# The down product of a bidirectional encoder layer: the first pair's weight parts at two places modulo 256 bytes, and its first matmul whole

## The chip, the cores and the metric

The kernel runs on one core of a Trainium2 chip. The metric is the device time of one execution in microseconds (us). It is measured several times; the median of three runs of the kernel before is 824.79 us. One more execution was taken with the profiler, and all views of the profile and the trace below come from it.

TensorE multiplies a stationary operand of 128x128, which a weight load puts into the array, with a moving operand of up to 512 columns. The profile shows the two as separate instructions: PE is the matmul, PEld the weight load. DVE is VectorE, ACT is ScalarE, POOL is GpSimd, and SP is SyncE, which starts the loads of weights.

## The reference

The kernel computes one layer of an encoder for 512 rows (tokens) of 1024 values. A mixing part (retention and a gated spatial unit) comes first; the change concerns the feed-forward part at the end:

```python
def _conv_gated_mlp(h, w_up, conv_w, conv_b, w_down):
    hid = h @ w_up
    c = hid.shape[-1]
    hid = lax.conv_general_dilated(
        hid, conv_w.reshape(CONV_W, 1, c), window_strides=(1,),
        padding=((CONV_W // 2, CONV_W // 2),),
        dimension_numbers=('NWC', 'WIO', 'NWC'), feature_group_count=c) + conv_b
    a, b = jnp.split(hid, 2, axis=-1)
    return (jax.nn.gelu(a) * b) @ w_down
...
        h2 = _rmsnorm(x, g_pre_ffn)
        x = x + _rmsnorm(_conv_gated_mlp(h2, w_up, conv_w, conv_b, w_down), g_post_ffn)
```

Here h is 512 x 1024, w_up is 1024 x 5632, w_down is 2816 x 1024, and all is float32. The last matrix product, with w_down, is called the down product.

## The kernel before

**Two parts for each number.** Every float32 operand is split into a high part, rounded to the matmul's format, and a low part, the rest (`split`, lines 89 to 91: ScalarE writes the high part in line 84, VectorE subtracts in line 91). A product a x w is then three matmuls: high x high, high x low, low x high. So matmuls come in threes throughout.

**Weights.** All weights lie in DRAM as 146 blocks of 128 x 1024 values. `w_get` hands them out in order and keeps some blocks ahead of the use; SyncE loads a block into one of four raw buffers, ScalarE and VectorE write the parts into slots. There are nine slots of 128 x 1088 values (`slot`, lines 128 and 129), used in turn. A slot is a little larger than a block needs, so that its content can begin at an offset, `at`, given in values of 4 bytes. A row of a slot is 4352 bytes, 17 times 256, so the slots all begin at the same place modulo 256 bytes; the blocks that hold activations are 2048 bytes, 8 times 256. In the program as built, slots and activation blocks alike begin at 64 modulo 256. The place of an operand modulo 256 bytes is therefore 64 plus four times its offset:

- the first up products, called early (`w_block`, line 144; L949 calls the three matmuls of L229 to L231): offset 16, both parts at 128;
- the products of `Pair` (`w_form`, lines 174 to 177; `product`, L688), which the gates, u and the up product use: the low part has offset 16, place 128, and the high part has offset 528 or 560, place 128 or 0. u's first four forms have 560; u's later forms and the first four of the first gate have 528, all later ones 560;
- the down product (`w_down`, L197, and `w_block`, L144): offset 48, both parts at 0;
- activations and what is derived from them: 64.

**The order of the matmuls.** In `Pair.product` and in the early products the weights are stationary and the activations move. In the down product it is the other way: activations are stationary and the weight parts move. A `Pair` runs two 128 x 512 output blocks with seven products of quarter size each in place of eight; its products are 256 columns wide. Between them stand whole up blocks with 512 columns (L957).

**The down product.** The output is made in two halves of 512 columns. Of the 22 row blocks of w_down, 18 are taken in nine pairs (`DP`); the other four are `whole` blocks, two for each half. For a pair, `w_down` writes a slot pair for the unit "q" (three quarters of the weight block pair, as they are) and one for the unit "t" (four sums and differences of quarters, which VectorE makes in L190 to L195). The tile of the high part is named dh, that of the low part dl. `products` (L1077) then runs seven units, each for two halves of 128 rows and three matmuls, 42 matmuls of 256 columns a pair, into seven sums in PSUM. `add_whole` (L1098) adds the whole blocks, L1109: in the first half they follow pairs 4 and 6, in the second they come at the end. After each half VectorE combines the seven sums (`steps`, L1122 to L1129 and L1171 to L1179). At the very end, rows are scaled and written out, four row blocks in the order 0, 2, 1, 3 (L1207 to L1238).

**What the change touches.** `w_down`'s offset, L197, and the split of the first matmul in `products`, L1089 to L1095: where `lead` is set (the first half), the first matmul of all is issued as two, one of 16 columns and one of 240, with the same stationary operand. `lead` also caps how far `w_get` looks ahead in the last pair (L1080).

Of the kernel before, what the change touches and what calls it, by code (L numbers as in the profile page):

```python
# [32 lines left out]
DOWN0 = NW - NF  # L33
DP = 9
# [15 lines left out]
def tile_block(ctx: ExitStack, tc, xT, x, wall, par, cs, wsp, bsp, gpost, gpre, gffn, out):  # L50
    nc = tc.nc
# [6 lines left out]
    def nm(s):  # L58
        uid[0] += 1
        return f"{s}_{uid[0]}"  # L60

    def blk(dt=F32, n="blk", shape=(P, S)):
        return sb.tile(list(shape), dt, tag="blk", bufs=NBLK, name=nm(n))
# [4 lines left out]
    def tmp(n="tmp", shape=(P, S)):  # L68
        return sb.tile(list(shape), F32, tag="tmp", bufs=6, name=nm(n))
# [7 lines left out]
    def ps(shape=(P, S)):  # L77
        return pp.tile(list(shape), F32, tag="ps", name=nm("ps"))
# [4 lines left out]
    def copy(o, i):  # L83
        nc.scalar.activation(out=o, in_=i, func=AF.Copy)  # L84

    def as32(t):
        return t.bitcast(F32)

    def split(hi, lo, src):
        copy(hi, src)  # L90
        return nc.vector.tensor_sub(lo, src, as32(hi))  # L91
# [7 lines left out]
    i = 0  # L99
    while i < NW:  # L100
# [7 lines left out]
        elif i == UP0 + 2 * COUPLES[0][0]:  # L108
# [3 lines left out]
            i = UP0 + 2 * COUPLES[-1][1] + 2  # L112
# [12 lines left out]
    def raw_tile():  # L125
        return sb.tile([P, 1024], F32, tag="raw", bufs=4, name=nm("raw"))

    def slot(n, at=0, w=1024):
        return sb.tile([P, 1088], F32R, tag="w4", bufs=9, name=nm(n))[:, at : at + w]
# [51 lines left out]
    def w_down(form, i):  # L181

        if form == "q":
            raw = w_raw["q"] = raw_tile()
            nc.sync.dma_start(raw, wall[i])
            raw = raw[:, : 3 * 256]
        else:
            b, raw = w_raw["q"], raw_tile()
            two = "p (n c) -> p n c"
            nc.vector.tensor_tensor(  # L190
                out=raw[:, :512].rearrange(two, n=2), in0=b[:, :512].rearrange(two, n=2),
                in1=b[:, None, 768:].to_broadcast([P, 2, 256]), op=ALU.add,
            )
            nc.vector.tensor_add(raw[:, 512:768], raw[:, :256], b[:, 256:512])
            nc.vector.tensor_add(raw[:, 768:], raw[:, 512:768], b[:, 512:768])  # L195
        w = 768 if form == "q" else 1024
        hi, lo = slot("dh", 48, w), slot("dl", 48, w)  # L197
        if w_behind:
            copy(hi, raw)
            with tc.issue_after(w_behind[0]):  # L200
                nc.vector.tensor_sub(lo, raw, as32(hi))
        else:
            w_low[form, i] = split(hi, lo, raw).ins
        return hi, lo
# [4 lines left out]
    def w_size(u):  # L209
        return 2 if u[0] in ("blk", "q", "t") else 1  # L210

    def w_next():
        u = units[w_pos[1]]
        w_ready[w_pos[1]] = w_unit(u)
        w_pos[1] += 1
        return w_size(u)

    def w_get(look=LOOK, most=99):

        i = w_pos[0]  # L220
        w_pos[0] += 1
        room = 2 * look + (2 if w_size(units[i]) == 2 else 0)
        n = sum(w_size(u) for u in units[i : w_pos[1]])
        while w_pos[1] < len(units) and (w_pos[1] <= i or n + w_size(units[w_pos[1]]) <= min(most, max(room, 9 if look == LOOK else 0))):
            n += w_next()
        return w_ready.pop(i)
# [53 lines left out]
    for k in range(KD):  # L280
# [6 lines left out]
        wh, wl = w_get(1 if k < 4 else LOOK)  # L287
# [11 lines left out]
        for m in range(8):  # L299
            c = slice(m * P, (m + 1) * P)  # L300
# [78 lines left out]
    for m in range(8):  # L379
        t = blk(n="qkraw")  # L380
# [8 lines left out]
    for t in range(NT):  # L389
# [4 lines left out]
            start=True,  # L394
            stop=True,
# [252 lines left out]
    for n, acc in enumerate(t_group()):  # L648
        if n < 2:
            for k in (n + 2, n + 6):  # L650
                t = tmp("xT")
# [93 lines left out]
    for j in range(KD // 2):  # L745
        p = Pair(AF.Gelu_apprx_tanh, lambda: blk(n="u"), scale=rbc)
# [204 lines left out]
    def up_block(between=None):  # L951
        (wh, wl), o = w_get(), ps()
        for k in range(KD):
            if between and k == KD // 2:
                between()
            c = slice(k * P, (k + 1) * P)
            mm3(o, wh[:, c], wl[:, c], *h2(k, slice(0, S)), k == 0, k == KD - 1)  # L957
        return o
# [90 lines left out]
    i = 0  # L1049
    while i < NF:  # L1050
        if i in couples:
            p = Pair(None, lambda: tmp("c"), h2, h2forms)
            p.part1()
            o = [up_block()]
# [5 lines left out]
        else:  # L1060
            o = []
# [12 lines left out]
    M1, M2, M3, M5, M6, M7, M4, M8 = range(8)  # L1074
    whole = []

    def products(m, j, steps={}, lead=False):  # L1077
        for n, (unit, at, act) in enumerate(UNITS):
            if n in (0, 3):
                wh, wl = w_get(most=9 if lead and j == DP - 1 else 99)  # L1080
            if j == 0 and n not in m:
                m[n] = ps()
            f = slice(at * 256, (at + 1) * 256)
            ah, al = dforms[j][act]
            for t in range(2):
                c = slice(t * P, (t + 1) * P)
                o = m[n][:, t * 256 : (t + 1) * 256]
                for i, (a_, w_) in enumerate(((ah, wh), (ah, wl), (al, wh))):
                    first = j == t == i == 0  # L1089
                    cuts = (0, 16, 256) if lead and first and n == 0 else (0, 256)  # L1090
                    for p, q in zip(cuts, cuts[1:]):
                        nc.tensor.matmul(  # L1092
                            o[:, p:q], a_[:, c], w_[:, f][:, p:q], start=first and p == 0,
                            stop=j == DP - 1 and i == 2 and n not in (M2, M3, M4), skip_group_check=True,
                        )  # L1095
            steps.get(n, lambda: None)()

    def add_whole(m, t, g, w, last=False, banks=(0, 1)):  # L1098
# [16 lines left out]
    m = {}  # L1115
# [10 lines left out]
    def after4(yy=yy):  # L1126
# [4 lines left out]
    steps = {  # L1131
        M1: lambda: copy(e1, m[M1]),
        M2: lambda: v.tensor_add(c11, m[M2], e1),
        M3: lambda: copy(e3, m[M3]),
        M6: lambda: v.tensor_add(uu, m[M6], e1), M7: after7,
    }
    for j in range(DP):
        products(m, j, steps if j == DP - 1 else {}, True)
        if j + 1 < DP:
            with tc.issue_after(w_low["t", DOWN0 + j + 1]):  # L1140
                for kind, i in {0: later[:1], 1: later[1:3], 2: later[3:4], 3: later[4:6], 4: later[6:7], 5: later[7:]}.get(j, ()):
                    if kind == "w":
                        whole.append(two_parts(gp[2 * DP + i], i > 1))
                    else:
                        down_forms(i)
        if j in (3, 5):
            w = w_get()
            for t in range(NT):
                add_whole(m, t, j // 2 - 1, w, j == 5)
            if j == 5:  # L1150
                copy(c22, m[M8])
# [16 lines left out]
    m = {n: m[o] for n, o in ((M1, M8), (M2, M1), (M3, M2), (M5, M3), (M6, M6), (M7, M5), (M4, M7), (M8, M4))}  # L1168
# [10 lines left out]
    steps = {M1: lambda: copy(e1, m[M1]), M6: after6, M7: after7}  # L1179
    for j in range(DP):  # L1180
        products(m, j, steps if j == DP - 1 else {})
        if j == 0:
            w_behind.clear()
            after4()
        if 1 < j < 2 + NT:
            first_share(j - 2)
# [20 lines left out]
    for t in (0, 2, 1, 3):  # L1207
# [12 lines left out]
        for i, (b, e) in enumerate((((M2, e1), (M3, xx)), ((M4, uu), (M8, yy)))[t // 2]):  # L1220
            f, h = slice((t % 2) * 256, (t % 2 + 1) * 256), slice(i * 256, (i + 1) * 256)
# [139 lines left out]
```

## Time and profile before

| | |
|---|---|
| median of three runs | 824.79 us (823.5 to 825.1) |
| the profiled execution's own time | 824.38 us |
| its span, first to last instruction | 822.6 us |
| mean granted clock of TensorE | 0.998 |
| down product, start of the first matmul to start of the last | 702.49 to 814.13 us |
| from there to the end of the span | 8.5 us |

How to read it: the span is what the trace covers, and 1.8 us of the profiled execution lie around it. The granted clock is the share of TensorE's clock that the chip let through; 1.00 is full. A step is the time from the start of one matmul to the start of the next. The chain of work that ended last follows the last instruction back to what released it, step by step; where it names TensorE, the time between two entries is made of such steps. In the table by window, a matmul that only reaches into the window is counted too.

### The profile page before, as it was taken

The page shows a single profiled execution, that of the slowest core. Times are in us where ns is not written, and L with a number is a line of the kernel's source. Part 1 is how long each engine was busy: PE and PEld are TensorE (multiplying, and loading weights), DVE is VectorE, ACT ScalarE, POOL GpSimd, SP SyncE. Part 2 cuts the span into 40 slices and gives each one's busy share as a digit, 9 for nine tenths or more (in the row PEclk, how much of TensorE's full clock was granted, in tenths as well). Part 3 has the DMA queues.
Part 4 walks back from the last instruction along what each step waited for, and adds up shares of the span by engine and source line. Part 5 has one row for each costly group of instructions (what it writes and reads, how often), then busy time and mean ns, then how long its engine had stood idle before and what let it go on. Part 6 is the DMA issues. An engine that isn't in the chain of part 4 may idle for free.

```text
span 822.6 us, 13205 instructions
## 1 busy us (share of the span) xinstructions
PE 812.9 (99%) x5153; PEld 733.7 (89%) x5153; DVE 658.5 (80%) x1076; ACT 431.2 (52%) x733; POOL 103.9 (13%) x108
## 2 busy tenths in 40 slices
PE   9999999999999999999999999999999999999996
PEld 7888888888999999999988898999999998999995
DVE  7579897878898787767765589679899899898956
ACT  6636445536665444444444566456566566555532
POOL 0100000103221111132221211111111100000002
PEclk9999999999999999999999999999999999999999
DMA  8733222213233333223359111233333341334334
GB/s 287 255 116 103 77 78 77 77 52 93 75 105 127 103 103 102 80 101 103 125 165 364 64 58 50 100 103 103 103 103 103 103 154 53 102 103 128 105 129 129
DMA packets 29247, 93.76 MB, mean 114 GB/s; under 512 B 3392, under 2 KB 4032, under 8 KB 29184
## 3 DMA queue, kind: packets, MB, share of 16 engines
q1 hardware_dynamic: 26784, 86.58, 31.9%
q0 software_dynamic: 1968, 6.03, 2.5%
q8 instruction: 40, 0.66, 0.3%
q10 hardware_dynamic: 432, 0.30, 0.1%
q14 instruction: 23, 0.19, 0.1%
HBM read 88.19 MB, written 4.72 MB: 113 GB/s over the span
## 4 chain that ended last, share of the span: by engine, by line
PE 97%; issue 1%; POOL 1%; DMA 0%; DVE 0%; POOLq 0%; ACT 0%; ACTq 0%; DVEq 0%
PE ps L688 23%; PE ps L229 13%; PE ps L230 13%; PE ps L231 12%; PE ps L1092 11%; PE ps L493 5%; PE ps L494 5%; PE ps L495 5%; PE ps L842 2%; PE ps L844 2%; PE ps L843 2%; PE ps L1109 2%; PE ps L767 1%; PE ps L293 1%; PE ps L618 0%
## 5 line engine op out<-in xcount | busy, mean ns | idle before, releaser
L91 DVE TENSOR_TENSOR wl<-raw,wh 128x1024 fp32r<-128x1024 f32 (+1 forms) x93 | 109.2, 1183 | 48.3 <-PE ps L688 24.2
L84 ACT ACTIVATE wf<-raw 128x512 fp32r<-128x512 f32 x140 | 85.1, 626 | 98.5 <-PE ps L230 40.2
L91 DVE TENSOR_TENSOR wf<-raw,wf 128x512 fp32r<-128x512 f32 x140 | 110.9, 807 | 26.1 <-ACT wf L84 24.9
L688 PE MATMUL ps<-sh,wf 128*128 128x256 f32 x640 | 118.7, 277 | 0.0
L84 ACT ACTIVATE wh<-raw 128x1024 fp32r<-128x1024 f32 (+2 forms) x95 | 93.0, 989 | 33.0 <-DMA raw<-wall 13.0
L688 PEld LDWEIGHTS ps<-sh,wf 128*128 128x128 f32 x640 | 100.7, 188 | 0.9 <-ACT gh L84 0.2
L229 PE MATMUL ps<-h2h,wh 128*128 128x512 f32 (+1 forms) x256 | 93.2, 364 | 0.0
L230 PE MATMUL ps<-h2l,wh 128*128 128x512 f32 (+1 forms) x256 | 93.1, 364 | 0.0
L231 PE MATMUL ps<-h2h,wl 128*128 128x512 f32 (+1 forms) x256 | 92.7, 362 | 0.0
L688 PE MATMUL ps<-sl,wf 128*128 128x256 f32 x320 | 88.5, 276 | 0.0
L493 PE MATMUL ps<-wh,xh 128*128 128x512 f32 x192 | 75.1, 391 | 0.0
L494 PE MATMUL ps<-wl,xh 128*128 128x512 f32 x192 | 74.9, 390 | 0.0
L495 PE MATMUL ps<-wh,xl 128*128 128x512 f32 x192 | 74.9, 390 | 0.0
L171 POOL TENSOR_TENSOR raw<-raw,raw 128x512 f32<-128x512 f32 x20 | 34.1, 1703 | 239.3 <-DVE raw L169 185.9
L688 PEld LDWEIGHTS ps<-sl,wf 128*128 128x128 f32 x320 | 60.1, 188 | 0.8 <-issue 0.2
L231 PEld LDWEIGHTS ps<-h2h,wl 128*128 128x128 f32 x256 | 48.3, 188 | 7.7
L229 PEld LDWEIGHTS ps<-h2h,wh 128*128 128x128 f32 x256 | 48.2, 188 | 6.9
L230 PEld LDWEIGHTS ps<-h2l,wh 128*128 128x128 f32 x256 | 48.1, 188 | 6.5
L688 PE MATMUL ps<-xh,wf 128*128 128x256 f32 x288 | 53.4, 278 | 0.0
L84 ACT ACTIVATE dh<-raw 128x768 fp32r<-128x768 f32 (+1 forms) x36 | 33.9, 949 | 28.7 <-PE ps L1092 16.4
L1092 PE MATMUL ps<-dh,fl 128*128 128x256 f32 x168 | 47.3, 281 | 0.0
L1092 PE MATMUL ps<-dh,fh 128*128 128x256 f32 x168 | 47.3, 281 | 0.0
(322 smaller groups left out, 2071.6 us busy)
## 6 DMA issues: line engine op xcount, KB each, us to landing
raw<-wall SPq DMA_DIRECT2D x145, 512.0 KB, 3.5
x<-x SPq DMA_DIRECT2D x22, 256.0 KB, 5.5
xT<-xT SPq DMA_DIRECT2D x8, 256.0 KB, 5.2
x<-x POOLq DMA_DIRECT2D x8, 256.0 KB, 2.6
xT<-xT POOLq DMA_DIRECT2D x4, 256.0 KB, 3.9
out<-zs SPq DMA_DIRECT2D x3, 256.0 KB, 3.3
cs<-cs SPq DMA_DIRECT2D x2, 256.0 KB, 4.3
gpm<-gpost POOLq DMA_DIRECT2D x2, 256.0 KB, 3.8
```

The lines of the kernel that those rows point to most:

```text
L84: nc.scalar.activation(out=o, in_=i, func=AF.Copy)
L91: return nc.vector.tensor_sub(lo, src, as32(hi))
L171: nc.gpsimd.tensor_tensor(out=w_raw["T2"], in0=w_raw["T1"], in1=w_raw["B22"], op=ALU.add)
L229: nc.tensor.matmul(o, ah, bh, start=start, stop=False)
L230: nc.tensor.matmul(o, ah, bl, start=False, stop=False)
L231: nc.tensor.matmul(o, al, bh, start=False, stop=stop)
L493: nc.tensor.matmul(acc[t], xh[k][:, c], wh[:, f], start=k == 0, stop=False)
L494: nc.tensor.matmul(acc[t], xh[k][:, c], wl[:, f], start=False, stop=False)
L495: nc.tensor.matmul(acc[t], xl[k][:, c], wh[:, f], start=False, stop=k == KD - 1)
L688: nc.tensor.matmul(o, w_[:, c], a_, start=first and k == n == 0, stop=k == 3 and n == 2, skip_group_check=True,)
L842: nc.tensor.matmul(o, ah, bh, start=k == 0, stop=False)
L1092: nc.tensor.matmul(o[:, p:q], a_[:, c], w_[:, f][:, p:q], start=first and p == 0, stop=j == DP - 1 and i == 2 and n not in (M2, M3, M4), s ...
```

## The change

In the first pair of the down product (both of its units, "q" and "t", in the first half) the high part begins at offset 16 of its slot instead of 48; its low part stays at 48. So there dh lies at 128 modulo 256 bytes and dl at 0. All other pairs keep both at 0. The first matmul of the down product is issued whole. The flag is renamed from `lead` to `one` and keeps its other use.

```diff
-        hi, lo = slot("dh", 48, w), slot("dl", 48, w)
+        hi, lo = slot("dh", 16 if i == DOWN0 else 48, w), slot("dl", 48, w)
...
-    def products(m, j, steps={}, lead=False):
+    def products(m, j, steps={}, one=False):
         for n, (unit, at, act) in enumerate(UNITS):
             if n in (0, 3):
-                wh, wl = w_get(most=9 if lead and j == DP - 1 else 99)
+                wh, wl = w_get(most=9 if one and j == DP - 1 else 99)
...
                 for i, (a_, w_) in enumerate(((ah, wh), (ah, wl), (al, wh))):
-                    first = j == t == i == 0
-                    cuts = (0, 16, 256) if lead and first and n == 0 else (0, 256)
-                    for p, q in zip(cuts, cuts[1:]):
-                        nc.tensor.matmul(
-                            o[:, p:q], a_[:, c], w_[:, f][:, p:q], start=first and p == 0,
-                            stop=j == DP - 1 and i == 2 and n not in (M2, M3, M4), skip_group_check=True,
-                        )
+                    nc.tensor.matmul(
+                        o, a_[:, c], w_[:, f], start=j == t == i == 0,
+                        stop=j == DP - 1 and i == 2 and n not in (M2, M3, M4), skip_group_check=True,
+                    )
```

## The prediction

> **What bounds the kernel now.** I read the page first, for the engine that sets the time.
>
> ```profile
> span 822.6 us, 13205 instructions
> ...
> PE   812.9 (99%) x5153; PEld 733.7 (89%) x5153; DVE 658.5 (80%) x1076; ACT 431.2 (52%) x733; POOL 103.9 (13%) x108
> ...
> PE 97%; issue 1%; POOL 1%; DMA 0%; DVE 0%; POOLq 0%; ACT 0%; ACTq 0%; DVEq 0%
> ```
>
> TensorE is 97% of the chain that ended last. So time is saved only where the next matmul starts sooner; the number that matters is the step from start to start, which the records' own durations, overlapping, don't show. The chain of waits in order of time does (start, length, line, count). Here it is for the last up products (L688), then for the down product (L1092 and L1109).
>
> ```profile
> 660.39 5.45 PE ps L688 x48
> ...
> 702.65 19.90 PE ps L1092 x169
> 722.55 5.65 PE ps L1109 x48
> 728.20 9.89 PE ps L1092 x84
> 738.10 5.65 PE ps L1109 x48
> 743.75 59.36 PE ps L1092 x504
> ```
>
> Both kinds are 128x256 matmuls. The reader is to divide: 59.36 / 504 = 117.78 ns a step in the down product, but 5.45 / 48 = 113.5 ns in the up product.
>
> Are the 4 ns a wait? A table by window gives TensorE's busy time, its count and the granted clock; the second window is the early up products (L949), the third the end of the retention's.
>
> ```profile
> 743.60:802.94 59.34, 59.34 (x506) 1.00 0.38 119
> 482.34:494.94 12.60, 12.60 (x109) 1.00 0.25 85
> 115.76:119.60 3.84, 3.84 (x34) 1.00 0.29 84
> ```
>
> No: it is busy for the whole of each window, at clock 1.00. Two of each count still run from before their window, so the early products step at 12.60 / 107 = 117.8 ns and the retention at 3.84 / 32 = 120.0 ns. The chain for the u products gives a fourth case:
>
> ```profile
> 213.51 5.45 PE ps L688 x48
> 218.96 1.75 PE ps L618 x16
> 220.71 0.86 PE ps L741 x2
> 221.57 38.11 PE ps L688 x336
> ```
>
> 38.11 / 336 = 113.42 ns. Beside these steps I set where the operands lie. A weight load runs under the product before it, so I call "relation" the place of the weights being loaded less the place of that product's moving operand, modulo 256 bytes. In the built program blocks and slots all begin at 64. In an up couple (weight offsets of 560 and 16 words) the relations of three products are 192, 64, 192, as in u's first 48. In the down product of before (activations at 64, both parts at 64 + 192 = 0) all are 64; so they are in the early products and in u's 336; in the retention they are 0. In short: 192, 64, 192 steps at 113.5, 0 steps at 120.0, and 64 has two rhythms, 113.4 and 117.8, either of which holds for hundreds of products. The weight loads show the rhythm too (shortest, median, longest, in ns; the last row has count, busy us, mean ns):
>
> ```profile
> L688 PEld LDWEIGHTS ps<-h2h,wf x192: 187/188/188, 516.5 to 676.4; 128*128 128x128 f32 x192
> L1092 PEld LDWEIGHTS ps<-dh,fh x168: 187/188/188, 703.2 to 792.6; 128*128 128x128 f32 x168
> L1092 PEld LDWEIGHTS ps<-dl,fh x168: 191/192/193, 703.3 to 792.7; 128*128 128x128 f32 x168
> L230 PEld LDWEIGHTS ps<-vl,sm 128*128 128x128 f32 x7 | 1.3, 192 | 0.0
> ```
>
> All loads take 188 in the fast rhythm, one in three takes 192 in the 117.8 one, all take 192 at 120.0. The first row holds 192 loads of all eight up couples, each begun after 512-wide products, and none is above 188: with 192, 64, 192 the fast rhythm was always there.
>
> **The change, part by part.** *Places.* In the first pair dh moves to 64 + 64 = 128 and dl stays at 0; under products of dh, dl, dh the relations become 192, 64, 192. That is the up couples' sequence, and it begins behind the same neighbour, a 512-wide product. I take their step, 113.42 ns by the longest row. The first pair has 7 units x 2 halves x 3 = 42 products: 42 x (117.78 - 113.42) = 0.18 us.
>
> *All that comes after it.* From the second pair on the relations are 64 again, with two rhythms on record. The pair leaves TensorE in the fast one. A step at relation 64 lies in each three of the fast sequence and doesn't break it, and u's 336 products are such steps alone. So I take 113.42 for the rest too. The line L1092 has 9 x 42 x 2 = 756 products and L1109 has 4 x 48 = 192, in all 948; behind the first pair 906: 906 x 4.36 = 3.95 us. The bounds: the gain is nothing if the rhythm of before comes back at once, and at 120.0 the 948 products lose 2.1 us.
>
> *The first matmul.* Split, it stands like this:
>
> ```profile
> 702.26 0.39 PE L231 MATMUL ps<-h2h,wl 128*128 128x512 f32 x1
> 702.49 0.39 PE L1092 MATMUL ps<-dh,fa 128*128 128x16 f32 x2
> 702.71 0.29 PE L1092 MATMUL ps<-dl,fa 128*128 128x256 f32 x1
> ```
>
> The two pieces take 702.71 - 702.49 = 0.22 us to the next product; whole it takes one step, 0.11 to 0.12. That removes one weight load and one matmul and saves 0.11 us, 0.10 at the least, unless the short piece is what keeps the down product off the 120 ns rhythm (a rival below). The sum so far is 0.18 + 3.95 + 0.11 = 4.24 us.
>
> *Who feeds TensorE.* The new cover is the lead of ScalarE and VectorE, since they must deliver up to 4 us earlier; no instruction, wait or DMA of theirs is added or moved, and the slot is as large as before. VectorE is nearly full in places (first row: busy us and count of TensorE, weight loads, VectorE, ScalarE, GpSimd), but TensorE paces it (the waits: us in all, times, longest):
>
> ```profile
> 722.40:743.60 21.20, 21.20 (x183) 21.20 (x182) 21.09 (x41) 10.43 (x15) 0.59 (x1) 1.00 0.29 94
> ...
> ACT dh L84 <- PE ps L1092: 16.4, 12, 1.8
> ...
> DVE dl L91 <- PE ps L1092: 3.3, 4, 1.9
> ```
>
> The parts wait for slots that TensorE frees. The thinnest lead that I find is behind the last products of the first half, where VectorE combines sums first:
>
> ```profile
> 760.72 0.68 DVE L1124 TENSOR_TENSOR c<-ps,uu 128x512 f32<-128x512 f32 x1
> 761.32 2.08 DVE L201 TENSOR_TENSOR dl<-raw,dh 128x1024 fp32r<-128x1024 f32 x2
> 765.61 0.28 PE L1092 MATMUL ps<-dl,fh 128*128 128x256 f32 x1
> ```
>
> The first of that row's two is done by about 761.3 + 1.2 = 762.5 and its first reader runs at 765.6, 3 us later. VectorE's run-up there is itself released by this half's sums and shifts with them, so only some 5 us of faster products, about 0.2 us, come off the 3. I cost this at nothing; without the cover it would take back the part of the 4 us that lies behind the stall.
>
> *The end.* The last quarter is VectorE's:
>
> ```profile
> 811.63 0.43 DVE L1222 TENSOR_TENSOR z<-ps,e 128x256 f32<-128x256 f32 x1 [0.28 <-PE ps L1109]
> ...
> 814.40 0.74 DVE L1201 SCALAR_TENSOR_TENSOR zg<-zg,qr,x 128x512 f32<-128x512 f32 x1
> 815.06 0.15 DVE L1227 TENSOR_TENSOR q<-q 128x1 f32<-128x1 f32 x1
> 815.13 0.41 DVE L1222 TENSOR_TENSOR z<-ps,e 128x256 f32<-128x256 f32 x1
> ```
>
> The step at 811.63 is the last that waits for TensorE; the one at 815.13 starts as VectorE comes free. The some 25 products after 811.5 therefore give nothing: 25 x 4.36 = 0.11 us off, which leaves 4.24 - 0.11 = 4.1 us.
>
> **The sum.** The profiled execution took 824.38 us (its span 822.6), 0.41 under the median of the three runs shown, 824.79. 824.38 - 4.1 = 820.3, and 820.7 from the median: I forecast 820.5 us. About 0.2%, 1.6 us, is what a measurement of this kernel can tell from no change.
>
> **The rivals.** *Places don't matter.* The step would belong to the kind of product: the slow ones here stream weights and hold activations, the fast ones the other way. Then the edit of places does nothing, and the split's 0.11 us is left: 824.7. For it: all L1092 and L1109 steps are slow. Against it: the early products hold weights and stream h2 as the up couples do, at 117.8. The Trainium skill, "TensorE: Matmul & The Clock Gate", section "Step-by-step: what each phase is for", speaks for this rival: it gives TensorE two independent read ports, so that loading the next weights takes nothing from the running product's reads. By that rule places are free and only the 0.11 us would remain; the three steps at one clock and one width don't agree with it. Chance 0.10.
>
> *The rhythm falls back.* At the second pair, or later, relation 64 returns to 117.8. At the second pair it leaves 0.18 + 0.11 = 0.3 us: 824.5; each hundred products that it holds longer gives 0.44. For it: both slow groups at relation 64 began and stayed slow. Against it: u's 336 began after the pause of L741 and stayed fast to the end. No place of before shows a change from one relation to the other without a pause. Chance 0.10.
>
> *The down product goes to 120.0.* Here the moving operand changes its place, not the weights as in the up couples; if each change costs what relation 0 costs, and the rhythm then stays, all loads take 192. Or it starts so because the short piece is gone. 948 x (120.0 - 117.78) = 2.1, less 0.1 for the split, is 2.0 us more: 826.8. It is slower than before once the mean step passes 117.9 ns, and measurably so from about 119.6. For it: the retention shows such a rhythm, and before has no mixed places in a moving operand. Against it: the relation alone sorted the four cases above. Chance 0.13.
>
> **How the numbers follow.** The forecast has the remaining 0.67. Its own range is the three runs' (823.5 to 825.1) less 4.1, widened a little for the tail: 819.3 to 821.5. The full range runs on through a late fall-back and the first two rivals, to 824.9, and leaves out the third. Faster by over 0.2% is the forecast and 0.03 of the fall-backs, those that hold past some 350 products: 0.70; the same is 0.10 + 0.07 = 0.17; slower is 0.13.
>
> **What would show it.** Right: the chain's 504 products of L1092 in 57.2 us instead of 59.36, dl's loads at 188 with dh's, the first product one 128x256, and no idle time ahead of L1092. If dl's loads go back to 192 from some pair on, the rhythm fell back there; if from the first product on with dh's at 188, places don't matter; if dh's too are at 192, the third rival holds. Idle time at about 761 would show that feeding was costed too low. The forecast is wrong if the steps behind the first pair aren't near 113.4.

## The result, and the profile after

| | before | after |
|---|---|---|
| median of 20 executions each | 824.78 us (823.5 to 825.4) | 823.21 us (822.62 to 824.92) |
| ratio, 95% interval | | 0.9984 [0.9978, 0.9991] |
| the profiled execution, its span | 824.38, 822.6 us | 823.27, 821.5 us |

The change gains 1.6 us, not 4.1. All ratios here and below leave out two executions that took far longer, one of e10 (2042.9 us) and one of e11 (1166.8 us, granted clock 0.655). Lines of the changed kernel behind the edit stand three lower than before: the products are L1089, the whole blocks L1106, and VectorE's combining steps after the first half L1119 to L1132.

The page of the changed kernel, as far as it answers to the lines shown of before:

```profile
span 821.5 us, 13204 instructions
...
PE 810.4 (99%) x5152; PEld 730.1 (89%) x5152; DVE 658.0 (80%) x1076; ACT 430.6 (52%) x733; POOL 103.9 (13%) x108
...
PE 93%; DVE 2%; DMA 2%; issue 1%; POOL 1%; POOLq 0%; ACT 0%; DVEq 0%; ACTq 0%
```

TensorE's share of the chain that ended last fell from 97% to 93%; VectorE and loads of weights are now in it. The chain in order of time says where (start, length, what):

```profile
703.14 19.20 PE ps L1089 x168
722.34 5.44 PE ps L1106 x48
727.78 1.94 PE ps L1089 x17
...
753.51 3.44 DMA raw<-wall
...
757.65 0.68 DVE c L1130
...
761.71 0.69 DVE c L1121
762.45 39.73 PE ps L1089 x348
802.18 2.73 PE ps L1106 x24
```

Two things are to be seen. The step is there: 5.44 / 48 = 113.3 ns in the whole blocks, where before had 5.65 / 48 = 117.7. And the chain leaves TensorE at 729.7: it runs over loads of weights and VectorE's work, at the end its c of L1121, and comes back only at 762.45. The weight loads show the fast rhythm too (shortest, median, longest); dl's median was 192 before:

```profile
L1089 PEld LDWEIGHTS ps<-dh,fh x168: 186/188/189, 703.6 to 792.0; 128*128 128x128 f32 x168
...
L1089 PEld LDWEIGHTS ps<-dl,fh x168: 187/188/192, 703.7 to 792.2; 128*128 128x128 f32 x168
```

Now the timeline of the changed kernel around that place (start, length, engine; in brackets the idle time ahead and what ended it):

```profile
757.04 0.69 DVE L190 TENSOR_TENSOR raw<-raw 128x512 f32<-128x512 f32 x1 [1.63 <-DMA raw<-wall]
...
757.65 0.68 DVE L1130 TENSOR_TENSOR c<-ps,e 128x512 f32<-128x512 f32 x1
...
758.25 0.95 DVE L91 TENSOR_TENSOR dl<-raw,dh 128x768 fp32r<-128x768 f32 x1
...
759.45 0.68 DVE L1132 TENSOR_TENSOR uu<-ps,e 128x512 f32<-128x512 f32 x1
...
760.88 0.28 PE L1089 MATMUL ps<-dh,fl 128*128 128x256 f32 x1
...
761.71 0.68 DVE L1121 TENSOR_TENSOR c<-ps,uu 128x512 f32<-128x512 f32 x1
...
762.45 0.39 PE L1089 MATMUL ps<-dh,fh 128*128 128x256 f32 x1 [1.29 <-DVE c L1121]
```

TensorE is in the second half's first pair. The products at 758.39, 760.19 and 762.45 each open a new sum, and each needs a PSUM bank whose old sum, of the first half, VectorE must have read (L1130, L1132, L1121). VectorE does so late: it waits 1.63 us for a load of weights, to make the sums of unit t in L190, and its reading of the banks stands behind that in its queue. The three steps into these products take 0.29, 0.43 and 1.57 us in place of 0.11, and the step behind each takes 0.22.

The product at 762.45 is the 505th of the down product. In before it starts at this row:

```profile
761.96 0.28 PE L1092 MATMUL ps<-dh,fh 128*128 128x256 f32 x1
```

With it the down product falls in two parts (starts of the first, the 505th and the last product, from the traces; the last column is of run e15, below):

| us | before | after | e15 |
|---|---|---|---|
| first to 505th | 702.49 to 761.96: 59.47 | 702.98 to 762.45: 59.47 | 703.44 to 760.72: 57.28 |
| 505th to last | 761.96 to 814.13: 52.17 | 762.45 to 812.78: 50.33 | 760.72 to 810.92: 50.20 |

So the first part gained nothing, to the hundredth of a microsecond, and the second gained 1.84 us. Of the 1.84 the two profiled executions keep 1.11 (824.38 less 823.27): the down product starts 0.49 us later, and the end takes 0.2 us longer. The medians keep 1.57; executions of one kernel differ by more than these remainders.

### The profile page after: what moved, and what is told of

It is laid out like the page before. It is cut to its first block, busy times and chain, and to the rows that moved or that the text cites. A ratio compares the mean times of both kernels' runs of the same rounds, so it can differ in the third digit from the quotient of the medians.

```text
span 821.5 us, 13204 instructions
## 1 busy us (share of the span) xinstructions
PE 810.4 (99%) x5152; PEld 730.1 (89%) x5152; DVE 658.0 (80%) x1076; ACT 430.6 (52%) x733; POOL 103.9 (13%) x108
## 4 chain that ended last, share of the span: by engine, by line
PE 93%; DVE 2%; DMA 2%; issue 1%; POOL 1%; POOLq 0%; ACT 0%; DVEq 0%; ACTq 0%
PE ps L688 23%; PE ps L229 13%; PE ps L230 13%; PE ps L231 12%; PE ps L1089 7%; PE ps L494 5%; PE ps L493 5%; PE ps L495 5%; PE ps L844 2%; PE ps L843 2%; PE ps L842 2%; DMA raw<-wall 2%; PE ps L1106 1%; PE ps L767 1%; PE ps L293 1%
## 5 line engine op out<-in xcount | busy, mean ns | idle before, releaser
L1089 PE MATMUL ps<-dh,fh 128*128 128x256 f32 x168 | 46.7, 278 | 1.5 <-DVE c L1121 1.3
L1089 PE MATMUL ps<-dl,fh 128*128 128x256 f32 x168 | 46.4, 276 | 0.0
```

The source lines that it names most:

```text
L1089: nc.tensor.matmul(o, a_[:, c], w_[:, f], start=j == t == i == 0, stop=j == DP - 1 and i == 2 and n not in (M2, M3, M4), skip_group_check= ...
```

## The experiments

Two questions were open. What sets TensorE's step: the places, the split, or something else? And why does VectorE read the banks late? The theory on the first was that of the prediction, that the places of the first pair set the rhythm for all that follows; its rivals were the split, and any change of place. On the second the theory in the end was the order of VectorE's queue; the rivals were too much work on VectorE and too few buffers for loads. Diffs are against the changed kernel, and ratios against before, run on the same chip. Where an edit adds lines, the line numbers move by one to four.

**e1: the places alone.** The first matmul is split as in before.

```diff
+                    first = j == t == i == 0
+                    cuts = (0, 16, 256) if lead and first and n == 0 else (0, 256)
...
```

> The first matmul stays split in 16 and 240 columns, and only the first pair's high parts move to offset 16. Theory: the places of the first pair, not the split, choose the rhythm of the rest. Then the steps in the first pair are near 117, those behind it 113.3, TensorE stands still for about 2 us around 760 us as in the changed kernel, and the time is the changed kernel's 823.2 plus at most 0.1 us. Rival: the short first piece holds TensorE in the slow rhythm; then all steps are 117.8, there is no standstill, and the time is 824.8 as before.

823.4 us, ratio 0.9985 [0.9977, 0.9994]. Its chain (the first line shown is pairs 3 and 4):

```profile
728.67 9.52 PE ps L1092 x84
...
762.62 39.73 PE ps L1092 x348
```

9.52 / 84 = 113.3 ns, and a standstill of TensorE again, ending at 762.62. The places alone set the fast rhythm. The split costs what its rows said: from the first product to the first dl product it is 0.22 us with it and 0.12 without. The standstill is a little shorter than in the changed kernel: the 505th product starts 762.62 - 703.72 = 58.90 us after the first, there 59.47. The next run says why.

**e2: the whole first matmul alone.**

```diff
-        hi, lo = slot("dh", 16 if i == DOWN0 else 48, w), slot("dl", 48, w)
+        hi, lo = slot("dh", 48, w), slot("dl", 48, w)
```

> The first matmul is whole, and all parts stay at offset 48. Theory (the places choose): all steps 117.8, no standstill, 0.1 us less than before, 824.7. Rival (the whole first matmul chooses): steps of 113.3 behind the first products, a standstill of about 2 us around 760, about 823.2.

823.36 us, ratio 0.9984 [0.9975, 0.9993]: the same time as with the places, and neither view had that. The windows of its trace ahead of 762 and behind 764 us (width, TensorE's busy time and count, clock):

```profile
744.00:762.00 18.00, 18.00 (x155) 1.00 0.42 133
764.00:782.00 18.00, 18.00 (x161) 1.00 0.34 112
```

Two of each count run from before the window: 18.00 / 153 = 117.6 ns ahead, 18.00 / 159 = 113.2 behind. Between them lies this row:

```profile
763.00 0.38 PE L1089 MATMUL ps<-dh,fh 128*128 128x256 f32 x1 [0.19 <-DVE c L1121]
```

A short pause of TensorE, and behind it the fast rhythm, with no place changed. If the pause did it, a kernel without the pause must stay slow; e12 below was made for that.

Why is there a pause at all, with TensorE as slow as in before? Because the program as built has another order of VectorE's instructions once the first matmul is whole. The traces of before and e1 (split) show one order from 50 us ahead of the down product to the standstill, those of the changed kernel and e2 (whole) another. Here it is in before, then in the changed kernel (L195 makes the last sum of a unit t and frees a raw buffer; L1030 makes a sum of activations):

```profile
740.90 0.42 DVE L195 TENSOR_TENSOR raw<-raw,raw 128x256 f32<-128x256 f32 x1
741.23 0.42 DVE L1030 TENSOR_TENSOR gp<-gp,fs 128x256 f32<-128x256 f32 x1
```

```profile
741.93 0.42 DVE L1030 TENSOR_TENSOR gp<-gp,fs 128x256 f32<-128x256 f32 x1
742.27 0.42 DVE L195 TENSOR_TENSOR raw<-raw,raw 128x256 f32<-128x256 f32 x1
```

Counted from the first product, this L195 starts at 38.41 us in before and at 39.29 in the changed kernel, and the load that follows it at 38.89 and 39.77, both 0.88 us later. The c that frees the last bank (L1124 or L1121) starts at 58.23 in before and 58.17 in e1, but at 58.73 in the changed kernel and 58.98 in e2. So the split alone brings c forward by 0.56 us at fast products and by 0.75 at slow ones. In e2 the bank is free 58.98 + 0.74 = 59.72 us after the first product (0.74 is 762.45 - 761.71, from the rows of the changed kernel above); without a wait the product would come at 59.36 (e12, below). That is the pause.

**e3: dh at 128 in all pairs.**

```diff
-        hi, lo = slot("dh", 16 if i == DOWN0 else 48, w), slot("dl", 48, w)
+        hi, lo = slot("dh", 16, w), slot("dl", 48, w)
```

> The changed kernel with the high parts of all nine pairs in both halves at offset 16, the whole blocks unchanged. Theory: with the moving operand changing its place by 128 bytes from product to product there is no fast rhythm, and it is the return to one place that is fast: steps of about 117 in L1089 throughout, 113.3 in L1106 at most, no standstill or a short one, about 824.5. Rival (the forecast's own rule, that 192, 64, 192 is fast and only needs time to settle): 113.3 from the second pair on, and the standstill as in the changed kernel, 823.2.

825.5 us, ratio 1.0007 [0.9997, 1.0016]. Pairs and whole blocks, one behind the other:

```profile
703.22 19.66 PE ps L1089 x168
722.88 5.45 PE ps L1106 x48
```

19.66 / 168 = 117.0 ns in the pairs, whose places are mixed; 113.5 in the whole blocks, which have one place. Mixed places are themselves slow when it is the moving operand that changes. Fast is what follows them. Behind the standstill, whose last step is 1.56 us, the second half's mixed pairs go on at 117.8 ns (336 steps from 764.70), so the mixed places too have more than one step.

**e6, e7, e8: other places for all.** Both parts of all down blocks at one offset (16, 32 or 0 in place of 48), so the relation is 192, 128 or 0 throughout.

```diff
-            at = 48 if i >= DOWN0 else 16 if UP0 <= i < UP0 + EARLY else 0
+            at = 16 if i >= DOWN0 else 16 if UP0 <= i < UP0 + EARLY else 0
...
-        hi, lo = slot("dh", 16 if i == DOWN0 else 48, w), slot("dl", 48, w)
+        hi, lo = slot("dh", 16, w), slot("dl", 16, w)
```

> The changed kernel with all parts of the down product, whole blocks too, at offset 16: relation 192 from start to end, and the moving operand never changes its place. Theory (a step is slow only where the relation is 0 or where it is 64 and was entered without a pause; a moving operand that changes its place is slow as well): 113.3 from the first product on, a standstill of about 2 us near 760, 823.0 to 823.3. Rival (only relation 64 has a fast rhythm): near 117 or 120 until the end, 824.8 or more.

> The changed kernel with all parts of the down product at offset 32: relation 128 throughout, which no kernel so far has. With relation 0 at 120.0, 192 at 117.8 and 64 at 113.3 or 117.8, the theory that the place of the load against the stream decides has no rule for it beyond lying between 113.3 and 120.0, the same from the first product to the last; if it is 113.3 from the start, it needs no first pair at another place.

> The changed kernel with all parts of the down product at offset 0: relation 0 throughout. If the relation alone chooses at 0, as the retention suggests, all steps are 120.0 and the down product takes 2 us longer than before the change. If the rows of the retention are slow for another reason, 117.8 or 113.3.

e6: 825.52 us, ratio 1.0002 [0.9993, 1.0011]. e7: 827.79 us, and e8: 827.87 us, one execution of each. The chains' first lines, of e6, e7 and e8:

```profile
703.26 19.79 PE ps L1089 x168
```

```profile
703.93 20.16 PE ps L1089 x168
```

```profile
703.50 20.15 PE ps L1089 x168
```

Divided by 168 these are 117.8, 120.0 and 119.9 ns. The three steps are a matter of places alone: kernel, width and clock (1.00) are the same. Relation 0 costs 120.0 as in the retention, before and behind the pause near 764. Relation 128 costs 120.0 up to its pause (a step of 0.79 us) and 118.7 behind it (336 steps from 766.44). Relation 192 by itself is slow, and a pause of about 0.6 us at 763 left it at 117.8: in these traces only 64 reaches 113.3. Two of e6's ten executions, of which there is no trace, took 823.2 and 823.4 us, so whether relation 192 can be faster stays open. The time of a weight load is no sign of the step at every relation: in e6 the loads of dh and dl took 187 or 188 ns at steps of 117.8.

**e9: two places in the early up products.** There the weights are stationary, so it is the stationary operand that is mixed.

```diff
-            hi, lo = slot("wh", at), slot("wl", at)
+            hi, lo = slot("wh", 48 if at == 16 else at), slot("wl", at)
```

> The changed kernel with the high parts of the four early up blocks at offset 48 and their low parts at 16, so that their 192 products of 256 columns have the relations 192, 64, 192 with the weights stationary, as the up couples have. Theory (with stationary weights this sequence is always fast): their steps fall from 117.8 to 113.4, 192 x 4.4 = 0.85 us, and all that follows shifts: 822.4. Rival (that stretch is bound by the norms on VectorE and ScalarE, or TensorE's pace there is not the places'): steps of 117.8, or pauses of the same length, 823.2.

823.48 us, ratio 0.9985 [0.9976, 0.9994]: no gain on the changed kernel. The first 24 early products step at 113.9 ns instead of 118.0; those behind the transposes of L909 do not follow: the last 107 step at 118.9, against 117.8 in the changed kernel. So this mixed sequence isn't always fast where the stationary operand changes its place.

**e4: two of VectorE's sums on GpSimd.** For the activations of the later pairs, two of the four sums of L1027 to L1030.

```diff
-        v.tensor_sub(a[:, T0], a[:, T0], a[:, T1])
-        v.tensor_add(a[:, T1], b[:, T0], s_[:, T1])
+        if j >= EAGER:
+            nc.gpsimd.tensor_tensor(out=a[:, T0], in0=a[:, T0], in1=a[:, T1], op=ALU.subtract)
+            nc.gpsimd.tensor_tensor(out=a[:, T1], in0=b[:, T0], in1=s_[:, T1], op=ALU.add)
+        else:
...
```

> The changed kernel with two of the four sums of down_forms (those that make S3 and S4) on GpSimd for the four forms that are made during the down product: eight operations of 0.42 us, 3.4 us, less for VectorE between 707 and 745 us. Theory: the standstill of 2.2 us around 760 comes from VectorE being full from 703 to 745 and so reading the first half's sums late, and TensorE waits for their PSUM banks; then it shrinks below 1 us and the time falls to 821 to 822. Rival: VectorE only waits for loads of weights there, 0.6, 2.0 and 1.6 us, and these are as late as before; then the standstill stays at about 2 us and the time at 823.2.

831.94 us, ratio 1.0087 [1.0073, 1.0101]: a miss. The waits (us in all, times, longest):

```profile
DVE raw L190 <- DMA raw<-wall: 11.0, 6, 3.2
...
PE ps L1093 <- DVE c L1134: 4.8, 1, 4.8
```

The standstill grew to 4.8 us. The sums took 1.2 us each on GpSimd instead of 0.42, ScalarE waited for them, and the loads behind started later: VectorE waited 11.0 us for loads instead of 6.8. Behind it there is a second loss. The window that follows the standstill (width, TensorE's busy time and count, clock) shows TensorE at half its clock:

```profile
765.73:771.43 5.70, 5.70 (x26) 0.50 0.28 92
```

These 25 steps took 5.70 us in place of 25 x 113.3 ns = 2.83. Behind the standstill of 1.29 us in the changed kernel the clock stayed at 1.00.

**e10: the same two sums left out.** In the later pairs they are not made at all, so that products use values that were not combined; only the time is of interest.

```diff
-        v.tensor_sub(a[:, T0], a[:, T0], a[:, T1])
-        v.tensor_add(a[:, T1], b[:, T0], s_[:, T1])
+        if j < EAGER:
+            v.tensor_sub(a[:, T0], a[:, T0], a[:, T1])
+            v.tensor_add(a[:, T1], b[:, T0], s_[:, T1])
```

> The changed kernel without two of the four sums in down_forms for the four forms made during the down product (S3 and S4 are then the plain parts, so the output isn't the reference's): 8 x 0.42 = 3.4 us less work for VectorE between 707 and 745 us, and nothing for GpSimd. Theory: TensorE's standstill of 2.2 us around 760 is VectorE's lateness; then it shrinks to below 0.5 us and the time to 821.0 to 821.5. Rival: the lateness comes from the loads, which wait for slots that TensorE frees, and VectorE's own work doesn't matter; then 823.2 and a standstill of about 2 us.

823.51 us, ratio 0.9984 [0.9975, 0.9994]. VectorE has 3.4 us less to do, and the standstill is the same:

```profile
746.49 0.69 DVE L190 TENSOR_TENSOR raw<-raw 128x512 f32<-128x512 f32 x1 [2.67 <-DMA raw<-wall]
...
757.01 0.69 DVE L190 TENSOR_TENSOR raw<-raw 128x512 f32<-128x512 f32 x1 [1.56 <-DMA raw<-wall]
```

What VectorE saved it spent in waiting: at 746.49 it waits 2.67 us, where the changed kernel waited 0.57, and at 757 it is where it was. But this doesn't acquit VectorE's work, as the load that it waits for at 746.49 shows, in e10 and then in the changed kernel (start, length):

```profile
741.22 5.17 DMA raw<-wall
```

```profile
742.75 3.55 DMA raw<-wall
```

The saving did bring the load forward, from 39.77 us after the first product to 38.43. But there it took 1.6 us longer, beside two loads that GpSimd starts (L821), which ran from 740.78 to 747.03; in the changed kernel these two start at 743.01 and 744.19, behind the load's own start. So e10 leaves open whether less work would help. What it shows is that VectorE stands behind loads. The loads in turn wait for VectorE, which must have read a raw buffer before it is filled again; the first of SyncE's waits in the changed kernel from 700 to 765 us (us in all, times, longest):

```profile
SPq L185 <- DVE raw L195: 21.9, 4, 6.4
```

No load of weights there waits for TensorE.

**e5: a fifth raw buffer for loads.** To make room, one temporary and one activation block are taken away.

```diff
-NBLK = 60
+NBLK = 59
...
-        return sb.tile(list(shape), F32, tag="tmp", bufs=6, name=nm(n))
+        return sb.tile(list(shape), F32, tag="tmp", bufs=5, name=nm(n))
...
-        return sb.tile([P, 1024], F32, tag="raw", bufs=4, name=nm("raw"))
+        return sb.tile([P, 1024], F32, tag="raw", bufs=5, name=nm("raw"))
```

> The changed kernel with five raw buffers in place of four, paid for with one activation block (59 for 60) and one temporary (5 for 6). Theory of VectorE's own work: the waits of L190 for loads in 744 to 757 (4.2 us in the changed kernel) shrink to below 1 us, but VectorE was late already at 744, so the standstill shrinks by 1 to 2 us; 821.5 to 822.5, if the blocks taken away cost nothing elsewhere. Rival (the loads are not what makes VectorE late): the waits go and the standstill stays at 2 us.

829.09 us, ratio 1.0056 [1.0042, 1.0069]. The down product starts 5.8 us later (708.81), and TensorE still stands idle 1.73 us for L1121. L190 still waits for loads, 7.3 us in all (6.8 in the changed kernel). The time lost ahead of the down product hides what the buffer alone would do there: inconclusive.

**e11 and e15: the sums behind the banks.** The load that VectorE waits for at 757.04 is for products that run from 770.7 on, some 13 us later. So its three sums are put behind the last combining step, L1121, in VectorE's queue. Nothing else is changed. e15 is the same kernel as e11 again, and the views are of its trace.

```diff
+            with ExitStack() as behind:
+                if w_behind and i > DOWN0 + 12:
+                    behind.enter_context(tc.issue_after(w_behind[0]))
                 nc.vector.tensor_tensor(
...
```

> The changed kernel with one thing more: the three VectorE operations that make the sums of weights for the second half's third pair (L190, L194, L195 of its unit t, first used 13 us later) are ordered behind the last sum of the first half's results (L1121). In the changed kernel the first of them waits 1.6 us for its load ahead of VectorE's reads of the results, whose PSUM banks TensorE waits for. Theory (VectorE's order holds the banks): the standstill of 2.2 us falls below 0.3 us, the down product steps at 113.3 but for its first pair, and the time is 821.0 to 821.4. Rival (the loads and slots pace VectorE whatever its order): a standstill of 1.5 us or more stays, here or a few pairs later; 822.7 to 823.3.

> The changed kernel with VectorE's three sums of the coming pair set behind the first half's last combining step, once more, for a profile at full clock. Theory 'the standstill near 760 us is the order of VectorE's queue': no idle time of TensorE between the first and the last matmul of the down product, the 504 products of L1092 in 504 x 113.3 = 57.1 us, the last matmul about 2.2 us earlier than in the changed kernel (near 810.6 us), 821.1 us. Rival 'the sums only move the standstill': idle time of TensorE of a microsecond or more at another place (unit t's first products, near 768 us), and the time then gained elsewhere.

e11: 821.08 us, ratio 0.9955 [0.9941, 0.9968]. e15: 821.18 us, 0.9952 [0.9937, 0.9967]. The chain of e15:

```profile
703.60 19.20 PE ps L1092 x168
722.80 5.44 PE ps L1109 x48
728.24 9.52 PE ps L1092 x84
737.76 5.44 PE ps L1109 x48
743.20 57.12 PE ps L1092 x504
```

57.12 / 504 = 113.3 ns, with no standstill in it. Its timeline (L1124 is the changed kernel's L1121, L193 its L190):

```profile
759.22 0.68 DVE L1124 TENSOR_TENSOR c<-ps,uu 128x512 f32<-128x512 f32 x1
...
760.72 0.28 PE L1092 MATMUL ps<-dh,fh 128*128 128x256 f32 x1
...
761.82 0.68 DVE L193 TENSOR_TENSOR raw<-raw 128x512 f32<-128x512 f32 x1
```

VectorE reads the last bank 1.50 us ahead of the product that needs it. So the order of VectorE's queue is enough to make the standstill and to remove it, and this kernel beats both others.

**e12: the same order, with the whole first matmul alone.** e2's edit and e11's together.

> The same order of VectorE in the kernel whose first matmul is whole and whose parts all stay at offset 48. Theory (in that kernel a standstill turned the slow rhythm of relation 64 into the fast one): without the standstill all steps are 117.8 to the end, about 824.7. Rival (the whole first matmul brings the fast rhythm from the second half on): 113.3 behind 763 us all the same, about 823.0.

824.73 us, ratio 1.0001 [0.9992, 1.001]; the chain steps at 117.7 to 117.8 ns in each of its five lines from the first pair to the last. Without the pause, the kernel of e2 stays slow to the end. So its pause had set the fast rhythm, and the whole first matmul doesn't.

**e13 and e14: how little is enough.** Both are e11 with another first pair: in e13 only unit q's 18 products are mixed; in e14 both parts are at 128 in the first pair, so the place changes once and is never mixed.

```diff
-        hi, lo = slot("dh", 16 if i == DOWN0 else 48, w), slot("dl", 48, w)
+        hi, lo = slot("dh", 16 if i == DOWN0 and form == "q" else 48, w), slot("dl", 48, w)
```

```diff
-        hi, lo = slot("dh", 16 if i == DOWN0 else 48, w), slot("dl", 48, w)
+        at = 16 if i == DOWN0 else 48
+        hi, lo = slot("dh", at, w), slot("dl", at, w)
```

> The changed kernel with VectorE's three sums of the coming pair set behind the first half's last combining step (as in the version that took 821.08 us), and with dh at 128 only in unit q of the first pair: 18 products with mixed places in place of 42. Question: how much of the mixed sequence does TensorE need to go over to the 113.3 ns step at relation 64? Theory 'a short mixed stretch is enough': the products behind the first 18 step at 113.3 to the end; against 821.08 us the 24 products of unit t gain 24 x (117.0 - 113.3) = 0.09 us, so 821.0 us. Rival 'it has to hold for some tens of products': with the pair's unit t at relation 64 the step goes back to 117.8, and since no standstill comes to change it, it stays there: 824.7 us, as the version with the whole first matmul alone and the same order of VectorE's work took (824.73).

> The same order of VectorE's work, but both parts of the first pair at 128 (relation 192 in all of its 42 products) and both at 0 from the second pair on (relation 64): the places change once, between two pairs, and are never mixed within a group of three. Theory 'any change of place into relation 64 sets the fast step': 117.8 ns in the first pair, 113.3 from the second on, 821.1 us, as the mixed first pair gives. Rival 'the mixed groups of three set it': relation 64 is entered from an even 117.8 and holds it to the end, 824.7 us.

e13: 820.86 us, ratio 0.9948 [0.9933, 0.9963]. e14: 824.72 us, ratio 0.9997 [0.9987, 1.0006]. First the window of e13's unit t in the first pair, then the 504 products of e14's chain:

```profile
705.25:707.97 2.72, 2.72 (x26) 1.00 0.00 0
```

```profile
743.87 59.36 PE ps L1093 x504
```

2.72 / 24 = 113.3 ns right behind 18 mixed products, and 59.36 / 504 = 117.8 after a change that was never mixed. The mixed groups of three set the rhythm, and six of them are enough; fewer weren't tried.

## Why the prediction was wrong

- **The failed step: "Who feeds TensorE", costed "at nothing", with "TensorE paces it" and a thinnest lead of 3 us.** The 3 us were measured to the readers of dl. The thin lead lay one row above, in a row that was quoted: VectorE's c (L1124) starts at 760.72 in before, and the changed kernel shows that the product which takes its bank can start 762.45 - 761.71 = 0.74 us after such a start, so at 761.46. In before it runs at 761.96: a lead of 0.50 us, not 3.
- **What the runs showed in its place.** VectorE's part didn't shift with TensorE. It goes by its loads (3.44 us each, about one in each 5 us), and these wait for VectorE: its last three L190 ahead of c lie 5.5 and 5.1 us apart in before (745.43, 750.94, 756.05), and in the changed kernel too (746.39, 751.92, 757.04). With the queue's order as in before, c comes at 58.17 us after the first product though the products are fast (e1), against 58.23. That "no instruction, wait or DMA of theirs is added or moved" was wrong as well: the whole first matmul moved VectorE's order, and c came at 58.73. Without the wait the 505th product comes 57.28 us after the first (e15), with it 58.73 + 0.74 = 59.47, as in before. The difference, 2.19 us, is the missing gain: the faster products used up the lead of 0.50, and with c 0.50 later the standstill came to the whole 2.19. That idle time near 761 would show this was named as the sign; its price was put at nothing.
- **The fast step behind the first pair: right.** 113.3 ns forecast as 113.4, and held to the end. e15, where nothing stands in the way, takes 107.48 us from the first product to the last; before takes 814.13 - 702.49 = 111.64. The gain, 4.16, was forecast as 4.24 before the tail.
- **The first pair at 113.4: wrong, but small.** It steps at 117.0 (42 steps of the trace; e3's 168 pair products do the same), so its 0.18 us became 0.03. The reason given, that the relation alone sorted the cases, fell with it: 192, 64, 192 steps at 113.5 in the up couples, where the stationary operand changes its place, at 117.0 or 117.8 here, where the moving one does (e3), and at 118.9 in e9's last early products, where again the stationary one does.
- **The reason for the rest was incomplete.** A mixed stretch sets the fast rhythm (e1, e13); a change of place doesn't (e14); a pause can, at relation 64 (e2 against e12). At relation 0 and 192 a pause changed nothing (e8, e6), at 128 it took the step from 120.0 to 118.7 (e7). That the rest was fast thus came true by a reason that holds only in part. Why is not settled: no run shows what TensorE does differently in the two rhythms.
- **The whole first matmul: right in its own row only.** It saves 0.1 us there and sets no rhythm (e12). But it moved VectorE's order, which was not foreseen and cost some 0.5 us at c. Between e1 and the changed kernel the executions show no difference (823.4 and 823.2 us).
- **The tail: right in kind.** From the last product's start to the end of the span are 8.7 us in the changed kernel, 8.5 before.
- **The rivals.** *Places don't matter* is refuted by e8: relation 0 in place of 64 costs 2 ns a step and nothing else differs. The Trainium skill, "TensorE: Matmul & The Clock Gate", section "Step-by-step: what each phase is for", gives TensorE two independent read ports. By that rule, as the prediction read it, the steps of e6, e8 and e15 would be equal; 117.8, 119.9 and 113.3 ns at one clock say otherwise. *The rhythm falls back* didn't happen; *the down product goes to 120.0* didn't either.

## What to carry to other kernels

When an engine becomes faster, list for each thing that it takes from another (data, a slot, a PSUM bank) the lead in the old trace, and compare the smallest with the whole gain up to that point, not with the gain of the last few microseconds. An instruction that waits for a load it needs much later must not stand in a queue ahead of one that frees a buffer: look for idle time ahead of it that costs nothing yet. Compare the order of each engine's instructions in the two traces, too: taking one matmul away here moved VectorE's. And where a step has several values at one clock, set the places of the operands beside it and test them one at a time.

## What the runs showed of the hardware

- 128x256 matmuls at one clock step at 113.3 to 120.0 ns, by the places of moving and stationary operand modulo 256 bytes: relation 0 at 120.0, 128 at 120.0 (118.7 behind a pause, e7), 192 at 117.8, mixed (192, 64, 192) in the moving operand at 117.0 (117.8 behind a standstill, e3), mixed in the stationary operand at 113.5 (up couples) or 118.9 (e9).
- Relation 64 has two rhythms, 113.3 and 117.8, and keeps the one that it is in for hundreds of products. It went over to the fast one behind 18 mixed products and behind a pause of under half a microsecond (the step into 763.00 in e2 took 0.47 us).
- Behind a standstill of TensorE of 4.84 us the granted clock was 0.50 for 5.70 us, and the steps took 0.21 us (e4). Behind standstills of 1.29 us (the changed kernel) and 1.73 us (e5) it stayed at 1.00.
- A 128x256 float32 sum took 0.74 to 2.30 us on GpSimd, 0.42 on VectorE; two of VectorE's dl of 128x768 that ran beside such sums took 1.49 and 1.50 us instead of 0.95 (e4). The Trainium skill, "SBUF — State Buffer", section "Who interferes with whom", has it that a VectorE instruction with two SBUF inputs contends with a GpSimd instruction that reads SBUF, since its second input comes through the read interface that the two share, and that the order of issue decides who blocks. These two rows, where the sum on GpSimd had started first, agree with it.
